# TensorE's order in a state-space layer: written out in the text, with two parts of a product between the steps of a unit

## The chip, the cores and the metric

The kernel runs on one core of a Trainium2 chip. A time is the device time of one execution in microseconds (us); the median of three timed runs stands for a kernel. The engines are named as in the profile: PE (TensorE, matmuls and transposes), DVE (VectorE), ACT (ScalarE), POOL (GpSimd) and SP (SyncE, which only issues DMAs here). Each engine works through its own list of instructions in order; an instruction waits until the results and buffers that it needs are there, and everything behind it on its engine waits too.

## What is computed

One inference step of a small decoder: a state-space layer (S5), then one attention layer. The change touches the S5 layer alone. Its core, for 1024 tokens of a prompt (and 8 x 8 tokens of samples, which start from a given state):

```python
def _s5_layer(x, h0_re, h0_im, ...):
    h = _rms_norm(x, g_pre)
    uz = h @ w_in
    u, z = uz[..., :SSM_WIDTH], uz[..., SSM_WIDTH:]
    y, hr, hi = _s5_scan(u, h0_re, h0_im, log_dt, a_re, a_im, b_re, b_im, c_re, c_im, d_skip)
    y = jax.nn.gelu(y)
    y = y * jax.nn.sigmoid(y @ w_glu + b_glu)
    y = y * jax.nn.silu(z)
    return x + _rms_norm(y @ w_out, g_post), hr, hi
```

`_s5_scan` splits the 1024 channels into 64 groups of 16. Each group has 64 complex states; for every token `h = lambda * h + B u` and `y = Re(C h) + d u`, with `lambda` and `B` made from `log_dt`, `a` and `b`.

## The kernel before

**Layout.** The tokens are laid out as 8 phases x 136 columns: eight neighbouring tokens make one chunk, there are 128 chunks of the prompt and 8 samples (`L` = 8, `W` = 136, `NC` = 128). So a row of a channel has 1088 columns, and the states are carried from chunk to chunk only, by a scan over 128 chunks.

**Products.** `u` and `z` are each made in eight column tiles of 128 channels (`KT` = 8), by `gemm_u(ft)` and `gemm_z(ft)`. One such product has three parts, by phases: `ACH = ((0, 3), (3, 3), (6, 2))` gives 408, 408 and 272 columns. A part is 24 matmuls into one bank `psmm`: for each of 8 slices of the inner dimension three (high x high, high x low, low x high, `mm3`, L147 to L149). ACT copies the bank out (L278, L281), and SP stores the finished row to DRAM (`u_d`, `zs_d`). Weights are split into `whi` (ACT, L140) and `wlo` (L141; DVE, or POOL for the odd tiles of z), two buffers each.

**Matrices of a column tile `ft`.** DVE makes `wb`, `ep` and `fk` from the parameters; PE transposes `ep` four at a time into the one bank `psm` (L342), ACT copies it to `et` (L343); eight small matmuls (L355) give `kp`, ACT copies them (L363), DVE adds the diagonal `dk` that POOL made, and SP places `kp` into `tg` with eight DMAs (L368). POOL makes the tables `cs` of cosines and sines (products `cs` and `m`, then their difference or sum), and four DMAs spread them into `cf` (L386). `cs` has one buffer, `cf` two.

**Units.** A column tile is worked on in three units of 3, 3 and 2 groups, named by their first group: (ft,0), (ft,3), (ft,6). A unit goes through the engines like this: PE multiplies the rows `ug` (read back from `u_d`) by `et` into a bank `psb` (L403); ACT copies the halves crosswise to `tb` (L410, L411); DVE multiplies `psb` by the cosines, POOL `tb` by the sines, DVE adds; DVE scans over the chunks (L418); ACT copies crosswise to `ts` (L425, L426); POOL multiplies `ts`, DVE `psb`, and DVE adds both into the states `hs`; PE adds up `tg` x `ug` (L435) and `fk` x `hs` (L436) in a bank `psa`; ACT puts GELU on it (L437) and behind the third unit SP stores the rows to `y_d`. Nearly all of DVE's and POOL's instructions are recorded on the one line of a helper (`tt`, L205).

**Buffers.** PSUM has two banks `psmm`, two `psa`, three `psb` and one `psm`. `hs` has two buffers, `tb` and `ts` share four.

**What sets the order.** All engines: a scheduler that runs a model of the program and takes, of what is ready, the instruction with the highest priority. The parts on matrices and units are in `tc.high_priority(OFA)`, the products are not, the weights have twice that priority. The text has the matrices of `ft`, then `gemm_u(ft + 2)`, the units of `ft`, and from `ft` = 3 on `gemm_z(ft - 3)`; the last three `gemm_z` stand behind the loads `yr` of the finished rows for the gated unit, and fill the time in which these are fetched and split (`yh` by ACT, L456, `yl` by DVE, L457). The gated unit's matmuls are the first with weights `whi_g`.

Of the kernel before, what the change touches and what calls it, by code (L numbers as in the profile page):

```python
# [10 lines left out]
F32 = mybir.dt.float32  # L11
# [4 lines left out]
ALU = mybir.AluOpType  # L16
# [29 lines left out]
LAG = 3  # L46
SHARE = (0.1, 0.2, 0.3, 0.4)
# [153 lines left out]
def s5_layer(tc, nc, io, wp, bank, cst, gains, ident, sgn, zs_d, u_d, y_d, s2):  # L201
# [5 lines left out]
    with ExitStack() as sx:  # L207
# [58 lines left out]
        def gemm(which, ft, evac, w=None):  # L266
            wh, wl = w or weights(which, ft)
            o = rows.tile([128, NTOK], F32, name=f"{which}t{ft}", tag="row")
            for c, (t0, m) in enumerate(ACH):
# [4 lines left out]
                evac(o[:, t0 * W : (t0 + m) * W], ps)  # L274
            return o

        def gemm_u(ft, w=None):
            nc.sync.dma_start(u_d[ft], gemm("u", ft, lambda o, ps: nc.scalar.activation(o, ps, AF.Copy), w))  # L278

        def gemm_z(ft):  # L280
            nc.sync.dma_start(zs_d[ft], gemm("z", ft, lambda o, ps: nc.scalar.activation(o, ps, AF.Copy)))  # L281

        gemm_u(0, w_first)
        gemm_u(1)


# [28 lines left out]
        units = 0  # L315

        for ft in range(KT):
            with tc.high_priority(OFA):
                gs = slice(ft * 8, ft * 8 + 8)

                pk = pk_all[:, gs, :]
                sb = tp.tile([128, 4, 8, GC], F32, name=f"sb{ft}", tag="sb", bufs=2)
                nc.scalar.dma_start(sb, io["s5_bc"][ft, :, 0:4])
                wb = tp.tile([128, 4, 8, GC], F32, name=f"wb{ft}", tag="wb")
                tt(V, wb[:, 0:2], sb[:, 0:2], bc(bc(wri[:, 0, gs], 2, GC), 1, 2), ALU.mult)
                tt(V, wb[:, 2:4], sb[:, 0:2][:, ::-1], bc(wri[:, 1:3, gs], 3, GC), ALU.mult)
                tt(V, wb[:, 0:2], wb[:, 0:2], wb[:, 2:4], ALU.add)
                V.tensor_scalar(sb[:, 2:4], sb[:, 2:4], sgn, None, op0=ALU.mult)

                ep = tp.tile([128, 8, L, GC], F32, name=f"ep{ft}", tag="ep")  # L330
                tm = tp.tile([128, 8, L, GC], F32, name=f"tm{ft}", tag="tm")
                lrv = pk[:, :, K_LR : K_LR + 8][:, :, ::-1]
                liv = pk[:, :, K_LI : K_LI + 8][:, :, ::-1]
                tt(V, ep, bc(lrv, 3, GC), bc(wb[:, 0], 2, L), ALU.mult)
# [54 lines left out]
            if ft + 2 < KT:  # L389
                gemm_u(ft + 2)  # L390
# [1009 lines left out]
```

## Time and profile before

| | |
|---|---|
| median of three runs | 1499.05 us (1498.17 to 1500.22) |
| profiled execution | 1500.17 us, its span 1498.4 us |
| PE busy over the span | 1415.8 us, 94% |
| DVE / ACT / POOL busy | 935.0 / 718.2 / 493.7 us |
| mean granted clock of PE | 0.982 |
| first unit's matmuls (L403) | 93.16 us from the span's start |
| last outputs of the last unit (L436) | end at 313.5 us |
| first matmul of the gated unit | 328.17 us |

The span runs from the first to the last instruction of the profiled execution; 1.8 us of its time lie outside it. The 94% of PE are a mean over very different stages: the attention behind 328 us is most of the span, and the change doesn't touch it. The layer's stretch, 93 to 328 us, has to be read by itself: how busy each engine is in it, and what ended each wait. In the rows, a bracket `[3.07 <-ACT ut L278]` says that the engine stood idle for 3.07 us ahead of this instruction, and that an ACT instruction of that line ended it. "x2" means two records taken together.

### The profile page before, as it was taken

The numbers are of one execution on the slowest core, as the hardware profiler recorded it, in microseconds if no ns is written. First come the engines' busy times: TensorE is split into PE (matmuls) and PEld (weight loads), VectorE is DVE, ScalarE is ACT, GpSimd is POOL, SyncE is SP. The second block draws the span as 40 slices with busy tenths as digits, with TensorE's granted clock in tenths as the row PEclk, the third lists the DMA queues.
The fourth block names the chain that finished last, engine by engine and source line by source line (L and its number), as shares of the span: only waits on it lengthen the run. The fifth ranks groups of instructions, "written<-read, shape, count | busy, mean of one in ns | idle before, by whom it ended". The sixth has DMA issues, their size and how long they took to land.

```text
span 1498.4 us, 26819 instructions
## 1 busy us (share of the span) xinstructions
PE 1415.8 (94%) x9648; PEld 1145.8 (76%) x9648; DVE 935.0 (62%) x1506; ACT 718.2 (48%) x1424; POOL 493.7 (33%) x473
## 2 busy tenths in 40 slices
PE   4987988899999989999999999999998999998997
PEld 3987978899977889999988877666565665565766
DVE  6877887758755531110122149897888888789545
ACT  5233454454434433332333347676665766576321
POOL 6556565325412132222111012433323233334200
PEclk9999999999999999999999999999999999999999
DMA  5345556674134252232288755979878686754026
GB/s 197 103 129 139 140 126 163 145 251 145 58 106 132 91 224 91 85 123 100 103 314 298 255 201 192 339 284 326 295 257 289 250 308 219 268 190 139 11 82 213
DMA packets 129670, 276.41 MB, mean 184 GB/s; under 512 B 21633, under 2 KB 66562, under 8 KB 129538
## 3 DMA queue, kind: packets, MB, share of 16 engines
q1 hardware_dynamic: 127234, 268.41, 54.0%
q10 hardware_dynamic: 2304, 6.29, 1.3%
q8 instruction: 76, 1.25, 0.3%
q14 instruction: 56, 0.46, 0.1%
HBM read 224.55 MB, written 39.35 MB: 176 GB/s over the span
## 4 chain that ended last, share of the span: by engine, by line
PE 75%; DVE 9%; POOL 5%; DMA 4%; issue 3%; ACT 2%; SPq 1%; DVEq 0%; POOLq 0%; ACTq 0%
PE psmm L147 7%; PE psmm L149 7%; PE psmm L148 7%; PE psqk L147 6%; PE psqk L148 6%; PE psqk L149 6%; PE psa L949 5%; PE psb L1182 5%; PE psb L1164 4%; PE psa L990 4%; PE psqk L1139 3%; PE psqk L1140 2%; DMA cf<-cs 2%; PE psa L147 2%; PE psa L149 2%
## 5 line engine op out<-in xcount | busy, mean ns | idle before, releaser
L1120 POOL TENSOR_TENSOR ql<-q,qh 128x256 fp32r<-128x256 f32 x64 | 62.5, 977 | 285.6 <-ACT qh L1119 246.5
L1141 ACT ACTIVATE F<-psqk,bp 128x384 f32<-128x384 f32 (+2 forms) x192 | 111.3, 580 | 64.6 <-PE psqk L1140 49.2
L1146 DVE TENSOR_TENSOR_SCAN F<-F,maskb 128x256 f32<-128x256 f32 (+3 forms) x128 | 131.2, 1030 | 14.0 <-ACT F L1141 13.6
L1149 POOL TENSOR_TENSOR S<-S,F 128x255 f32<-128x255 f32 (+3 forms) x64 | 100.8, 1574 | 115.7 <-DVE F L1148 22.5
L1142 ACT ACTIVATE S<-psqk,bp 128x384 f32<-128x384 f32 (+2 forms) x192 | 111.4, 583 | 22.7 <-PE psb L1164 22.6
L1164 PE MATMUL psb<-cst,S 128*128 128x128 f32 x576 | 96.7, 285 | 4.4 <-DVE og L1186 3.8
L1164 PEld LDWEIGHTS psb<-cst,S 128*128 128x128 f32 x576 | 67.3, 143 | 35.1 <-issue 20.5
L1148 DVE TENSOR_TENSOR_SCAN F<-F 128x384 f32<-128x384 f32 (+1 forms) x64 | 78.9, 1233 | 20.4 <-ACT F L1141 19.8
L1182 PE MATMUL psb<-at,vr 128*64 128x256 f32 (+1 forms) x640 | 90.0, 369 | 1.2 <-DVE at L1168 1.2
L949 PE MATMUL psa<-vp,sat 128*32 128x256 f32 x1024 | 86.1, 388 | 0.1
L1139 PE MATMUL psqk<-ks,qh 128*128 128x384 f32 (+2 forms) x192 | 77.4, 404 | 6.9 <-DVE ks L1104 5.2
L990 PE MATMUL psa<-kp,qbd 128*32 128x256 f32 x1024 | 75.5, 389 | 0.5 <-PE psb L1164 0.5
L1182 PEld LDWEIGHTS psb<-at,vr 128*64 128x64 f32 x640 | 46.7, 137 | 36.6 <-issue 10.3
L1168 DVE TENSOR_TENSOR at<-psb,maskb 128x384 f32<-128x384 f32 (+3 forms) x128 | 60.3, 478 | 21.3 <-PE psb L1164 20.7
L147 PE MATMUL psmm<-xh,whi_u 128*128 128x408 f32 (+1 forms) x192 | 65.3, 341 | 3.7 <-ACT ut L278 3.1
L147 PE MATMUL psmm<-x,whi_g 128*128 128x408 f32 (+1 forms) x192 | 66.6, 347 | 1.1 <-DVE gt L739 1.1
L943 DVE TENSOR_TENSOR_SCAN sF<-sF 128x513 f32<-128x513 f32 x32 | 44.4, 1388 | 36.1 <-ACT sF L940 35.8
L1139 PEld LDWEIGHTS psqk<-ks,qh 128*128 128x128 f32 x192 | 37.0, 193 | 37.8 <-ACT S L1142 12.8
L1140 PE MATMUL psqk<-ks,ql 128*128 128x384 f32 (+2 forms) x192 | 65.8, 344 | 0.0
L148 PE MATMUL psmm<-xl,whi_u 128*128 128x408 f32 (+1 forms) x192 | 65.4, 341 | 0.0
L149 PE MATMUL psmm<-x,wlo_g 128*128 128x408 f32 (+1 forms) x192 | 64.9, 338 | 0.2 <-DVE wlo_g L141 0.2
L148 PE MATMUL psmm<-x,whi_g 128*128 128x408 f32 (+1 forms) x192 | 65.1, 339 | 0.0
(452 smaller groups left out, 4234.6 us busy)
## 6 DMA issues: line engine op xcount, KB each, us to landing
kp<-cache_kT SPq DMA_DIRECT2D x128, 512.0 KB, 6.0
vp<-cache_v SPq DMA_DIRECT2D x128, 512.0 KB, 5.7
cf<-cs SPq DMA_DIRECT2D x32, 256.0 KB, 5.4
q<-q_d SPq DMA_DIRECT2D x128, 64.0 KB, 4.6
u_d<-ut SPq DMA_DIRECT2D x8, 544.0 KB, 2.8
ug<-u_d SPq DMA_DIRECT2D x64, 68.0 KB, 2.9
y_d<-gt SPq DMA_DIRECT2D x64, 68.0 KB, 2.4
zs_d<-zt SPq DMA_DIRECT2D x8, 544.0 KB, 4.5
```

What stands on the lines that cost most here:

```text
L147: nc.tensor.matmul(ps, sh, mh, start=(k == 0), stop=False)
L148: nc.tensor.matmul(ps, sh, ml, start=False, stop=False)
L149: nc.tensor.matmul(ps, sl, mh, start=False, stop=(k == n - 1))
L949: self.nc.tensor.matmul(po[32 * r : 32 * r + 32, 0:256], a[:, 32 * r : 32 * r + 32], rhs[:, r * 256 : (r + 1) * 256], start=start, stop=stop)
L990: nc.tensor.matmul(ps[32 * r : 32 * r + 32, half * 256 : half * 256 + 256], self.qbd[:, 2 * r + e, s, :], kt[:, :, 2 * r + e, :], start=(e ...
L1139: nc.tensor.matmul(ps[:, :m], qh[:, w], ks[:, c0 : c0 + m], start=True, stop=False)
L1141: nc.scalar.activation(F[:, c0 : c0 + m], ps[:, :m], AF.Sigmoid, bias=bp[:, 1, h : h + 1], scale=-0.125)
L1142: nc.scalar.activation(S[:, c0 : c0 + m], ps[:, :m], AF.Sigmoid, bias=bp[:, 0, h : h + 1], scale=0.125)
L1146: V.tensor_tensor_scan(fr, fr, self.maskb[:, 512 - m : 512][:, ::-1], 1.0, ALU.mult, ALU.max)
L1149: (Q if i % 2 else V).tensor_tensor(S[:, 0 : n - 1], S[:, 0 : n - 1], F[:, 1:n], op=ALU.mult)
L1164: nc.tensor.transpose(ps[:, j * 128 : (j + 1) * 128], S[:, (j0 + j) * 128 : (j0 + j + 1) * 128], self.ident)
L1182: nc.tensor.matmul(po[hs, o:256], self.vr[pi][:, j, hs], ats[hh][j // 4][:, j % 4, o:256], start=(j == 0), stop=(j == nj - 1))
```

## The change

A product becomes a generator that yields after each part, and the products stand in one list: u0, then the order of `FILLS`. From the first product to the end of the layer's units PE takes its instructions in the order of the text (`tc.manual_schedule` for PE alone); the other engines' order still comes from the scheduler, whose model now has PE's order given. `fill(n)` writes the next n parts. The work of a unit is split in two functions: `states` (the matmuls into `psb` and all up to `hs`) and `outputs` (the matmuls into `psa` and GELU). The loop goes over the 24 units: states of unit n, one part of a product, outputs of unit n - 2 (`ULAG` = 2), and behind the second and third unit of a tile one half of the next tile's matrices. In the first three tiles one more part stands ahead of the second half. `hs` has three buffers instead of two, `tb` and `ts` three instead of four.

```diff
+ULAG = 2
+FILLS = "u1 u2 z0 u3 u4 z1 u5 z2 u6 z3 u7 z4 z5 z6 z7".split()
...
-        def gemm(which, ft, evac, w=None):
+        def gemm(which, ft, w=None):
...
-                evac(o[:, t0 * W : (t0 + m) * W], ps)
-            return o
...
-        gemm_u(0, w_first)
-        gemm_u(1)
+                nc.scalar.activation(o[:, t0 * W : (t0 + m) * W], ps, AF.Copy)
+                if c == len(ACH) - 1:
+                    nc.sync.dma_start((u_d if which == "u" else zs_d)[ft], o)
+                yield
+        fills = chain(gemm("u", 0, w_first), *(gemm(n[0], int(n[1])) for n in FILLS))
+        st.enter_context(tc.manual_schedule(engines={mybir.EngineType.PE}))
+        def fill(n):
+            for _ in range(n):
+                next(fills, None)
+        fill(6)
...
-        for i in range(2):
+        for i in range(ULAG + 1):
...
-                    tb = work.tile([128, 3, NC], F32, name=f"tb{ft}_{g0}", tag="tb", bufs=4)
+            tb = work.tile([128, 3, NC], F32, name=f"tb{ft}_{g0}", tag="tb", bufs=3)
...
-                    hs = h_t[units % 2]
+            hs = h_t[(3 * ft + j) % (ULAG + 1)]
...
+        first = matrices(0)
+        fill(7)
+        ahead(first)
+        fill(1)
+        ahead(first)
+        nxt = None
+        for n in range(3 * KT + ULAG):
+            ft, j = divmod(n, 3)
+            if n < 3 * KT:
+                with tc.high_priority(OFA):
+                    states(ft, j)
+            if j == 1 and ft + 1 < KT:
+                nxt = matrices(ft + 1)
+            fill(1)
+            if n >= ULAG:
+                with tc.high_priority(OFA):
+                    outputs(*divmod(n - ULAG, 3))
+            if nxt and j:
+                if j == 2 and ft < 3:
+                    fill(1)
+                ahead(nxt)
+                nxt = nxt if j == 1 else None
...
-        for ft in range(5, 8):
-            gemm_z(ft)
+        for _ in fills:
+            pass
```

`matrices(ft)` holds the text of before in two halves: up to `fk`, with all eight transposes, and from the `kp` products to the loads `ug`. `ahead` runs one half at the high priority.

**How the order moves, first place: POOL at the first unit.** `m2` and `cs2` belong to tile 2's table, `dk1` to tile 1, `tb0_0` and `ts0_0` to the first unit; `wlo_z1` is a weight split. Before:

```order
L205 TENSOR_TENSOR m2_1370<-uu_569 128x512
L205 TENSOR_TENSOR tb0_0_966<-tb0_0_966,cf0_861 128x384
L205 TENSOR_TENSOR cs2_1369<-uu_569 128x512 x2
L205 TENSOR_TENSOR cs2_1369<-cs2_1369,m2_1370 128x512
L205 TENSOR_TENSOR ts0_0_977<-ts0_0_977,cf0_861 128x384
```

After:

```order
L207 TENSOR_TENSOR m2_1643<-uu_571 128x512
L207 TENSOR_TENSOR cs2_1642<-uu_571 128x512 x2
L207 TENSOR_TENSOR cs2_1642<-cs2_1642,m2_1643 128x512
L207 TENSOR_TENSOR m2_1643<-uu_571 128x512
L207 TENSOR_TENSOR dk1_1340<-cst_63,dcol_572 16x128
L207 TENSOR_TENSOR tb0_0_1114<-tb0_0_1114,cf0_1096 128x384
L207 TENSOR_TENSOR cs2_1642<-cs2_1642,m2_1643 128x512
L143 TENSOR_TENSOR wlo_z1_1398<-wraw_z1_1395,whi_z1_1397 128x1024
L207 TENSOR_TENSOR m3_1927<-uu_571 128x512
L207 TENSOR_TENSOR ts0_0_1124<-ts0_0_1124,cf0_1096 128x384
```

The first unit's `tb` has moved behind the first half of tile 2's table and `dk1`, and its `ts` behind the rest of the table and a weight split.

**Second place: PE at the end of column tile 3.** `psa` are outputs, `psb` states, `psm` transposes, `psmm` parts of a product; `hs` and `fk3` belong to tile 3's last unit, `et4` and `ug4` to tile 4's last, `ep5` to the matrices of tile 5. Before:

```order
L147 MATMUL psmm103_2525<-xh0_89,whi_z2_2520 128x408
L342 MATMUL psm92_2279<-cst_63,ep5_2267 128x128
L435 MATMUL psa83_2094<-ug4_2070,tg0_792 128x136
L436 MATMUL psa72_1808<-hs1_790,fk3_1597 128x136
L435 MATMUL psa72_1808<-ug3_1726,tg1_793 128x136
L436 MATMUL psa72_1808<-hs1_790,fk3_1597 128x136
L403 MATMUL psb86_2140<-ug4_2070,et4_1928 128x136 x2
L342 MATMUL psm92_2279<-cst_63,ep5_2267 128x128 x3
L148 MATMUL psmm103_2525<-xl0_92,whi_z2_2520 128x408
```

After:

```order
L151 MATMUL psmm89_2292<-xh0_89,wlo_z3_2288 128x408
L451 MATMUL psa90_2318<-ug3_1939,tg1_797 128x136
L452 MATMUL psa90_2318<-hs2_794,fk3_1808 128x136
L451 MATMUL psa90_2318<-ug3_1939,tg1_797 128x136
L452 MATMUL psa90_2318<-hs2_794,fk3_1808 128x136
L347 MATMUL psm91_2345<-cst_63,ep5_2339 128x128 x4
L347 MATMUL psm92_2351<-cst_63,ep5_2339 128x128 x4
L409 MATMUL psb93_2362<-ug4_2197,et4_2086 128x136 x2
L149 MATMUL psmm94_2382<-xh1_90,whi_z3_2287 128x408
```

Before, the small steps stood singly inside a part of a product; now they stand together between two whole parts, the two sets of transposes back to back.

**Third place: POOL in column tile 5**, with the table of tile 7. Before:

```order
L205 TENSOR_TENSOR ts5_0_2439<-ts5_0_2439,cf5_2323 128x384
L205 TENSOR_TENSOR tb5_3_2458<-tb5_3_2458,cf5_2323 128x384
L205 TENSOR_TENSOR cs7_2917<-uu_569 128x512 x2
L205 TENSOR_TENSOR cs7_2917<-cs7_2917,m7_2918 128x512
L205 TENSOR_TENSOR m7_2918<-uu_569 128x512
```

After:

```order
L207 TENSOR_TENSOR cs7_2958<-uu_571 128x512 x2
L207 TENSOR_TENSOR ts5_0_2478<-ts5_0_2478,cf5_2450 128x384
L207 TENSOR_TENSOR cs7_2958<-cs7_2958,m7_2959 128x512
L207 TENSOR_TENSOR tb5_3_2525<-tb5_3_2525,cf5_2450 128x384
L207 TENSOR_TENSOR m7_2959<-uu_571 128x512
```

The table's first products have moved ahead of the `ts` of unit (5,0). At the end of the layer PE has, behind the last `L436`, 95 matmuls of z products before the gated unit; behind the last `L452` it has 120.

## Rows read from the trace of the kernel before

**Rows 1.** By stretch: length; PE, PEld, DVE, ACT, POOL busy; clock; DMA share; GB/s.
```profile
93.00:310.20 217.20, 188.65 (x1290) 179.59 (x1289) 165.40 (x290) 100.73 (x228) 124.93 (x99) 0.96 0.57 139
131.00:290.50 159.50, 139.06 (x947) 132.11 (x946) 128.33 (x215) 73.16 (x168) 94.40 (x72) 0.96 0.62 148
...
313.30:328.20 14.90, 14.90 (x98) 14.89 (x98) 5.89 (x5) 7.00 (x9) 2.53 (x1) 1.00 0.86 252
...
225.00:250.00 25.00, 20.03 (x132) 19.15 (x131) 18.26 (x35) 9.71 (x23) 13.73 (x12) 0.86 0.63 159
```

**Rows 2.** PE's waits, 93 to 310.2 us: total, times, longest.
```profile
PE psa L435 <- ACT gt L437: 10.0, 4, 5.0
PE psa L436 <- DVE hs L205: 8.4, 4, 3.5
```

**Rows 3.** DVE's waits from 131 to 290.5 us, in the same columns.
```profile
DVE psb L205 <- ACT ts L426: 12.5, 12, 1.1
DVE hs L205 <- POOL ts L205: 4.9, 3, 3.4
DVE psb L205 <- ACT tb L411: 4.2, 10, 0.6
DVE psb L205 <- POOL tb L205: 4.1, 2, 3.2
DVE sb L328 <- DMA sb<-s_bc: 3.2, 2, 1.7
```

**Rows 4.** PE's instructions in order: start us, duration us, name, [idle before <- releaser].
```profile
66.17 0.35 PE L147 MATMUL psmm<-xh,whi_u 128*128 128x408 f32 x1
...
70.63 0.29 PE L147 MATMUL psmm<-xh,whi_u 128*128 128x272 f32 x1
...
73.65 0.35 PE L147 MATMUL psmm<-xh,whi_u 128*128 128x408 f32 x1
...
105.93 0.71 PE L147 MATMUL psmm<-xh,whi_u 128*128 128x408 f32 x1 [3.07 <-ACT ut L278]
...
312.89 0.39 PE L435 MATMUL psa<-ug,tg 128*128 128x136 f32 x2
313.12 0.39 PE L436 MATMUL psa<-hs,fk 128*128 128x136 f32 x2
...
328.17 0.35 PE L147 MATMUL psmm<-yh,whi_g 128*128 128x408 f32 x1
```

**Rows 5.** POOL's instructions at the start, and one of its waits (93 to 310.2 us).
```profile
98.76 1.00 POOL L205 TENSOR_TENSOR tb<-tb,cf 128x384 f32<-128x384 f32 x1
105.92 2.15 POOL L205 TENSOR_TENSOR cs<-uu 128x512 f32<-128x512 f32 x2 [6.16 <-DMA cf<-cs]
108.03 1.28 POOL L205 TENSOR_TENSOR cs<-cs,m 128x512 f32<-128x512 f32 x1
...
115.44 1.51 POOL L205 TENSOR_TENSOR dk<-cst,dcol 16x128 f32<-16x128 f32 x1
...
POOL cs L205 <- DMA cf<-cs: 18.9, 5, 6.2
```

**Rows 6.** DVE's instructions at the first and last units and at the reload.
```profile
99.80 0.57 DVE L205 TENSOR_TENSOR psb<-psb,tb 128x384 f32<-128x384 f32 x1 [3.87 <-POOL tb L205]
...
110.32 0.55 DVE L205 TENSOR_TENSOR hs<-psb,ts 128x381 f32<-128x381 f32 x1 [2.69 <-POOL ts L205]
...
126.42 0.42 DVE L205 TENSOR_TENSOR hs<-psb,ts 128x254 f32<-128x254 f32 x1 [0.37 <-POOL ts L205]
...
290.46 0.28 DVE L205 TENSOR_TENSOR kp<-kp,dk 16x128 f32<-16x128 f32 x1 [0.40 <-ACT kp L363]
...
293.76 0.42 DVE L205 TENSOR_TENSOR hs<-psb,ts 128x254 f32<-128x254 f32 x1 [0.43 <-POOL ts L205]
...
309.68 0.42 DVE L205 TENSOR_TENSOR hs<-psb,ts 128x254 f32<-128x254 f32 x1 [0.43 <-POOL ts L205]
...
327.42 1.29 DVE L457 TENSOR_TENSOR yl<-yr,yh 128x1088 fp32r<-128x1088 f32 x1 [1.18 <-ACT yh L456]
```

More of the change, by code (lines that the diff above doesn't have):

```diff
@@ new lines, in states @@
+        def states(ft, j):
+            g0, n = ACH[j]
+            pk, et, fk, tg, cof, sif = made[ft]
+            ug = rows_in[ft]
+            pg = bank("b")
+            for i in range(n):
+                nc.tensor.matmul(pg[:, i * W : (i + 1) * W], et[:, g0 + i, :], ug[:, g0 + i, :], start=True, stop=True)
+            pg3 = pg[:, : n * W].rearrange("p (a b) -> p a b", a=n)
+            gsl = slice(ft * 8 + g0, ft * 8 + g0 + n)
+            gl = slice(g0, g0 + n)
+            ta = pg3[:, :, 0:NC]
+            tb = work.tile([128, 3, NC], F32, name=f"tb{ft}_{g0}", tag="tb", bufs=3)
+            nc.scalar.activation(tb[0:64, :n], pg3[64:128, :, 0:NC], AF.Copy)
+            nc.scalar.activation(tb[64:128, :n], pg3[0:64, :, 0:NC], AF.Copy, scale=-1.0)
+            tt(V, ta, ta, cof[:, gl], ALU.mult)
+            tt(V, sst[:, gsl, :], pg3[:, :, NC:W], pk[:, gl, K_LH : K_LH + NS], ALU.add)
+            tt(Q, tb[:, :n], tb[:, :n], sif[:, gl], ALU.mult)
+            tt(V, ta, ta, tb[:, :n], ALU.add)
+            for i in range(n):
+                g = ft * 8 + g0 + i
+                V.tensor_tensor_scan(
+                    ta[:, i], rho[:, g : g + 1].to_broadcast([128, NC]), ta[:, i], 0.0, ALU.mult, ALU.add
+                )
+            hs = h_t[(3 * ft + j) % (ULAG + 1)]
+            ts = work.tile([128, 3, NC], F32, name=f"ts{ft}_{g0}", tag="tb", bufs=3)
+            nc.scalar.activation(ts[0:64, :n], ta[64:128], AF.Copy, scale=-1.0)
+            nc.scalar.activation(ts[64:128, :n], ta[0:64], AF.Copy)
+            tt(Q, ts[:, :n], ts[:, :n], sif[:, gl], ALU.mult)
+            nc.scalar.activation(hs[:, :n, NC:W], pk[:, gl, K_H0 : K_H0 + NS], AF.Copy)
+            tt(V, ta, ta, cof[:, gl], ALU.mult)
+            tt(V, hs[:, :n, 1:NC], ta[:, :, 0 : NC - 1], ts[:, :n, 0 : NC - 1], ALU.add)
+            tt(V, l1[:, gsl], ta[:, :, NC - 1], ts[:, :n, NC - 1], ALU.add)
+            started[ft, j] = hs
@@ new lines, in outputs @@
+        def outputs(ft, j):
+            g0, n = ACH[j]
+            gl = slice(g0, g0 + n)
+            pk, et, fk, tg, cof, sif = made[ft]
+            ug, hs = rows_in[ft], started.pop((ft, j))
+            if j == 0:
+                rows_out[ft] = work.tile([128, 8, W], F32, name=f"gt{ft}", tag="gt")
+            gt = rows_out[ft]
+            py = bank("a")
+            for i in range(n):
+                g = g0 + i
+                o = py[:, i * W : (i + 1) * W]
+                nc.tensor.matmul(o, tg[:, g, :], ug[:, g, :], start=True, stop=False)
+                nc.tensor.matmul(o, fk[:, g, 1:, :].rearrange("p a b -> p (a b)"), hs[:, i, :], start=False, stop=True)
+            nc.scalar.activation(gt[:, gl], py[:, : n * W].rearrange("p (a b) -> p a b", a=n), AF.Gelu_apprx_tanh)
+            if j == len(ACH) - 1:
+                ydst = y_d[ft].rearrange("(g c) (t n) -> t c g n", c=GC, t=L)
```

194 lines of the change are left out of this document (77 added, 117 removed).

## The prediction, before the result

> **What bounds the kernel now.** I read the stretches first. Between the first unit's matmuls (93 us) and the end of the last column tile but one or so (310.2 us) TensorE (PE) is busy for 188.65 of 217.2 us, VectorE (DVE) for 165.40, and nobody is full [rows 1]. So the question is who waits for whom. PE's own waits come next: the two largest are for GELU results that free its `psa` bank (10.0 us) and for the states `hs` from DVE (8.4 us) [rows 2]; both are ends of the chain of a unit, which runs PE, ACT, DVE, POOL, DVE, ACT, POOL, DVE, PE. PE stands because that chain is late, not because its own queue is badly filled. Then DVE's waits from the end of tile 1's `kp` to the start of tile 7's (131 to 290.5 us): 12.5 us for the copy `ts` and 4.2 us for the copy `tb`, both in small pieces, one for nearly every unit; and, in a few long pieces, 4.9 us for POOL's `ts`, 4.1 us for POOL's `tb`, 3.2 us for the load `sb` [rows 3]. The first kind lies inside a unit (scan, then copy by ACT, then multiply) and I call it structural; the second kind, 4.9 + 4.1 + 3.2 = 12.2 us, could go with another order. DVE is busy for 128.33 of these 159.5 us [rows 1]; with the structural waits, and some 2 us that no row names, that is 159.5 - 12.2 = 147.3 us, 24.5 us for a column tile. PE in the same window has 139.06 us of work [rows 1]. My reading: the chain through DVE sets the pace of the units, and the products fill PE beside it. What is left of the products runs behind the last unit: from 313.1 us to the first matmul of the gated unit at 328.17 us, without a gap (14.90 us busy of 14.90) [rows 1, 4].
>
> So the end of the layer is: time at which the last unit's outputs are through, plus the products still to do then. After that the order of the program is the same in both kernels, and I carry any difference through unchanged.
>
> **The change, part by part.**
>
> *The start (+1.3).* Before, POOL does the first unit's `tb` at 98.76 us, ahead of the table `cs` of tile 2, which it can only start at 105.92 us, after 6.16 us of waiting for tile 1's `cf` transfers to read the single `cs` buffer [rows 5]. After, four instructions of tile 2's table and tile 1's `dk` stand ahead of that `tb` on POOL (the first fence of the change). With the same landing, `tb` starts at about 105.92 + 2.15 (two products) + 1.28 (the difference) + 1.1 (one more product, half of the pair) + 1.51 (`dk`) = 112 us [rows 5], 13 us later. Behind it, the last step of the table and one weight split stand ahead of `ts`, some 5 us; the first `hs` comes at about 119 us where it came at 110.32 [rows 6]. PE in text order then stands at the first outputs for about 8 us, and everything behind waits: next unit's part, tile 1's transposes. Most of it is covered: DVE does tile 1's matrices while it waits, which before stood between the units, and its waits there (3.87 us ahead of 99.80, 2.69 us ahead of 110.32 [rows 6]) are partly the same idle time. Walking DVE's list with the durations of the trace I get the third unit's `hs` at about 128.9 us for 126.42, and tile 1's `kp` at the old time but with 1.3 us of work still behind it that was ahead of it. Bounds: 0 (all hidden) and 119 - 110.3 = 8.9 us (none). I take 1.3, since DVE has the work to hide it.
>
> *Six column tiles (-5).* From one `kp` to the next DVE has the same instructions. PE gets a state matmul of a unit out two units before its outputs, so DVE no longer waits for one; DVE had hardly such a wait before. What can shrink are the 12.2 us. They shrink where POOL's order is better: in tiles 1 to 3 the tables stand together between two units. In tiles 4 and 5 it gets worse: the two first products of `cs6` and `cs7`, 2.15 us a pair as at 105.92 [rows 5], and the rest of the table, stand ahead of a `ts` that DVE wants next (the third fence shows tile 5). Walked by hand: 1.0 us left in tile 1, 0.5 in tile 3, 1.8 in tile 4, 2.7 in tile 5, and 0 to 3 for `sb`, together 6 to 9 of the 12.2. The gain is 3.2 to 6.2 us; I take 5. Bounds: 12.2 (all gone), and a loss of 4.45 us, if one unit's matmuls come behind a whole part of a product at a point where DVE is waiting: a part of 408 columns took 70.63 - 66.17 = 4.46 us, one of 272 columns 73.65 - 70.63 = 3.02 us [rows 4].
>
> *PE's own budget.* A tile has three parts (4.45 + 4.45 + 3.0 = 11.9 us), or four in the first three tiles, and about 7 us of its own: 24 matmuls of the units at 313.12 - 312.89 = 0.23 us [rows 4], 5.5, and 16 smaller ones for the matrices, some 1.5. That is 18.9 or 23 us, less than the 24.5 of DVE. Both transposes of a tile now come back to back through the one `psm` bank, so PE waits for ACT's copy between them, at most 1.3 us a tile. With 5.6 us to spare in tiles 3 to 7 this costs nothing; without that cover (tiles 0 to 2, 1.5 us to spare) it would cost those 1.3 us once or twice. So PE still idles, about 5 us in each late tile, now always in one place, ahead of the outputs.
>
> *The last unit (-1).* Before, from tile 6's last `hs` (293.76 us) to the last output (313.12 + 0.39 us) went 19.75 us [rows 4, 6]. After, PE has behind that `hs`: outputs 0.9, states 0.45, a part 4.45, outputs 1.4, a part 3.0, outputs 1.4, a part 4.45, outputs 0.9, that is 17, and a wait of about 1.5 for the last `hs`, since DVE took 309.68 - 293.76 = 15.9 us for the same three units [rows 6]. I take 18.7, a gain of 1; bounds 0 and 2.7.
>
> *What is left behind the last output (+4.45).* The text hands out 14 parts before the first unit, one in each of 26 rounds and one more in three: 43 of 48. Five are left, two of z6 and three of z7, 120 matmuls where 95 stood before: 14.9 + 4.45 = 19.35 us. This is a count, with no range of its own. It hides the reload of the layer's result, whose last split stood at 327.42 us, about the end of z7 [rows 6], a little better than before.
>
> Sum: 1.3 - 5 - 1 + 4.45 = -0.25 us. The profiled execution took 1500.17 us with a span of 1498.4; the median of the three timed runs is 1499.05, 1.1 us below it. Against the median I get **1498.8 us**: no change. About 0.2%, 3 us, is what a measurement of this kernel can tell from none.
>
> **A rule to weigh.** The rows show two busy engines in the units, PE at 188.65 and DVE at 165.40 of 217.2 us [rows 1], and PE's waits naming DVE and ACT [rows 2]. The Trainium skill, page "Perfetto Trace Analysis", section "Identifying the Most-Contended Engine", holds the engine with the highest occupancy to be the one to work on first, though it adds that for TensorE busy time is a poor measure. By that rule PE would be the limit, and a better order on PE would pay its whole idle time. The sum above does not use it; it is the third rival below.
>
> **The rivals.**
>
> *DVE's avoidable waits go altogether (faster).* If the two units between states and outputs let POOL run ahead everywhere, all 12.2 us go and the start costs nothing: -12.2 - 1 + 4.45 = -8.7, about 1490 us. For it: POOL is busy for only 94.40 of 159.5 us [rows 1], so it has room. Against it: its order, and 18.9 us of waiting of POOL for `cf` transfers that still read the single `cs` [rows 5].
>
> *The units end no earlier (slower).* If the start's slip is not hidden, or PE's fixed order returns what POOL gives, the last output stays at 313.5 us or comes later, and the 4.45 us of products that were moved behind it are simply added: 1503.5 us, and up to 1508 with half of the 8.9 us of the start on top. The point at which it decides: units that get shorter by less than 4.45 - 3 = 1.5 us give a measurable loss. For it: PE in text order stands at every outputs that is late, and has nothing to put ahead of it. A worse form of it: the granted clock. After an idle time of 3.07 us the next matmul of 408 columns took 0.71 us instead of 0.35 [rows 4], and 225 to 250 us, with PE's longest wait of 5.0 us [rows 2], shows a granted clock of 0.86 [rows 1]. If every late tile's wait of 5 us does so, each brings some us of matmuls at 1.2 GHz; only where PE has no spare time does that reach the end, so I price it at 0 to 5 us inside this rival.
>
> *PE is the limit (much faster).* If PE's order alone made the waits, the 217.2 - 188.65 = 28.6 us of idle time go, less the first outputs' 8: 1499 - 20.6, about 1478 us. Against it: the waits end with DVE and ACT [rows 2]. The Trainium skill's rule above is this case.
>
> *The order does not matter.* PE's idle time is what DVE's pace leaves, wherever it lies; some 8 us at the start and five times 5 us are about 33, less what the units end earlier, near the 28.6 of before. This is the forecast by another way.
>
> **How the numbers follow.** No change (within 3 us of 1499): 0.38. DVE's waits gone: 0.25, PE the limit: 0.07, and a forecast whose tile term comes out at its better end, 0.02: faster 0.34. Units end no earlier: 0.20 without and 0.08 with the clock: slower 0.28. The range takes the first rival with some 4 us beyond it, as the ends of the terms (-12.2, -2.7) add up, 1485, and the slower one with its upper end, 1508. Left out are the limit by PE and tails on both sides, together about 0.2. The likeliest case's own range is 1496 to 1502.
>
> **What would show it.** In the changed kernel's profile: POOL's first `tb` near 112 us and PE's longest wait ahead of the first outputs, for `hs`; tile 7's `kp` on DVE at 285 to 288 us where it was 290.46 [rows 6]; the last outputs near 309 us and the first gated matmul near 328, with about 19.3 us of PE without a gap between; PE's waits by name nearly all `hs` from DVE, some `et` from ACT. If PE's idle time in the units falls well below 28 us, I am wrong about what bounds them; if the last outputs come at 313 us or later, the slower case holds; if the first gated matmul waits for anything but PE, the tail was mis-sized.

## The result, and the profile after

The changed kernel takes 1510.47 us (median of four timed runs, 1507.9 to 1512.5) against 1499.12 us of the kernel before on the same chip: a ratio of 1.0075, with a 95% interval of 1.0055 to 1.0094. It is slower by 11 us; the prediction said 1498.8, with a range that ended at 1508. The profiled execution took 1508.97 us with a span of 1507.2 us, 8.8 us more than the span before.

Where these 8.8 us come in is read off these marks in the two traces (us from the span's start; an `hs` is marked where DVE starts to write it):

| mark | before | after | difference so far |
|---|---|---|---|
| first states (psb <- ug, et) | 93.16 | 95.66 | +2.5 |
| hs of unit (6,6) | 293.76 | 291.21 | -2.55 |
| last outputs end | 313.5 | 314.8 | +1.3 |
| first gated matmul | 328.17 | 334.00 | +5.8 |
| the next PE wait of over 4 us | 540.19 | 549.22 | +9.0 |
| end of the span | 1498.4 | 1507.2 | +8.8 |

So DVE's chain is ahead of the old one near its end, and yet the layer ends later; then another 3.2 us are lost between the first gated matmul and the next long wait. The busy times of two stretches of the changed kernel, in the columns of [rows 1]:

```profile
95.60:314.50 218.90, 183.00 (x1255) 177.45 (x1249) 162.51 (x289) 99.00 (x227) 118.69 (x94) 0.94 0.53 135
314.50:334.00 19.50, 19.50 (x123) 19.49 (x122) 8.99 (x6) 8.92 (x12) 2.54 (x1) 1.00 0.87 283
```

In the units PE now stands for 218.9 - 183.0 = 35.9 us; before it was 28.6 [rows 1], in a stretch of nearly the same length. The second line is the tail: 19.5 us without a gap, where 14.9 stood [rows 1]. PE's waits of the changed kernel from 85 to 340 us, to be read against [rows 2]:

```profile
PE psm L347 <- ACT et L348: 28.4, 8, 8.0
PE psa L452 <- DVE hs L207: 3.7, 3, 2.4
PE psb L409 <- DVE wb L207: 2.6, 1, 2.6
PE psb L409 <- DMA ug<-u_d: 2.0, 1, 2.0
```

Of the two large waits of before, the one for GELU is gone, and the one for `hs` is down from 8.4 to 3.7 us. One new wait holds nearly all: at the second set of transposes of each tile PE stands for ACT's copy of the first set out of the one `psm` bank. One such place, in tile 3's matrices, from PE's list (start, duration, instruction, idle time ahead of it):

```profile
164.57 0.60 PE L347 MATMUL psm<-cst,ep 128*128 128x128 f32 x4
169.70 1.11 PE L347 MATMUL psm<-cst,ep 128*128 128x128 f32 x4 [4.53 <-ACT et L348]
170.61 1.11 PE L409 MATMUL psb<-ug,et 128*128 128x136 f32 x4
171.36 0.70 PE L149 MATMUL psmm<-xh,whi_z 128*128 128x408 f32 x1
```

The last two rows, the next unit's states and the next part of a product, did not need that copy; in the order of the text they had to stand behind it. Why the copy was late is in ACT's list at the same time:

```profile
165.42 0.49 ACT L429 ACTIVATE ts<-psb 64x384 f32<-64x384 f32 x1 [4.67 <-DVE psb L424]
165.92 0.48 ACT L430 ACTIVATE ts<-psb 64x384 f32<-64x384 f32 x1
166.43 0.49 ACT L416 ACTIVATE tb<-psb 64x384 f32<-64x384 f32 x1
166.93 0.48 ACT L417 ACTIVATE tb<-psb 64x384 f32<-64x384 f32 x1
167.43 1.06 ACT L142 ACTIVATE whi_u<-wraw_u 128x1024 fp32r<-128x1024 f32 x1
168.39 0.38 ACT L277 ACTIVATE ut<-psmm 128x272 f32<-128x272 f32 x1
168.67 0.39 ACT L453 ACTIVATE gt<-psa 128x272 f32<-128x272 f32 x1
168.95 0.22 ACT L432 ACTIVATE hs<-pk 128x16 f32<-128x16 f32 x1
169.05 0.60 ACT L348 ACTIVATE et<-psm 128x512 f32<-128x512 f32 x1
```

The copy takes 0.60 us, but eight other instructions stand ahead of it, and the first of them waits 4.67 us for a scan on DVE (L424). A transpose that needs nothing of the units has come to wait for the unit in work. In four of the eight places the copy stood behind a scan like this. The longest wait, 8.0 us ahead of tile 1's second transposes, had another reason: ACT also issues the loads of u's weights, and one of them could only go when POOL had split the weights of z out of the one buffer `wraw`.

```profile
109.48 2.33 POOL L143 TENSOR_TENSOR wlo_z<-wraw_z,whi_z 128x1024 fp32r<-128x1024 f32 x1
...
111.84 0.33 ACTq L222 DMA_DIRECT2D wraw_u<-a_win  x1
112.22 0.51 ACT L277 ACTIVATE ut<-psmm 128x408 f32<-128x408 f32 x1 [11.33 <-POOL wlo_z L143]
```

(Counted in the loop, three parts stand between a unit's states and its outputs, in the rounds n, n + 1 and n + 2, and not the two of the title.)

### The profile page after: what moved, and what is told of

Same layout as the page of the kernel before. It is cut to its first block, busy times and chain, and to the rows that moved or that the text cites. A ratio compares the mean times of both kernels' runs of the same rounds, so it can differ in the third digit from the quotient of the medians.

```text
span 1507.2 us, 26829 instructions
## 1 busy us (share of the span) xinstructions
PE 1417.8 (94%) x9648; PEld 1150.1 (76%) x9648; DVE 925.2 (61%) x1507; ACT 716.4 (48%) x1424; POOL 491.0 (33%) x473
## 4 chain that ended last, share of the span: by engine, by line
PE 73%; DVE 6%; DMA 4%; issue 2%; POOL 2%; ACT 2%; SPq 1%; DVEq 0%; POOLq 0%; ACTq 0%
PE psmm L149 6%; PE psmm L151 6%; PE psmm L150 6%; PE psqk L150 6%; PE psqk L149 6%; PE psqk L151 6%; PE psa L992 5%; PE psb L1225 5%; PE psa L1033 4%; PE psb L1207 4%; PE psqk L1182 3%; PE psqk L1183 2%; PE psa L149 2%; PE psa L151 2%; PE psa L150 2%
## 5 line engine op out<-in xcount | busy, mean ns | idle before, releaser
L1225 PEld LDWEIGHTS psb<-at,vr 128*64 128x64 f32 x640 | 46.7, 137 | 36.1 <-issue 10.5
L149 PE MATMUL psmm<-xh,whi_z 128*128 128x408 f32 (+1 forms) x192 | 66.7, 347 | 0.0
L986 DVE TENSOR_TENSOR_SCAN sF<-sF 128x513 f32<-128x513 f32 x32 | 44.4, 1388 | 36.1 <-ACT sF L983 35.8
```

The lines of the kernel that those rows point to most:

```text
L149: nc.tensor.matmul(ps, sh, mh, start=(k == 0), stop=False)
L1225: nc.tensor.matmul(po[hs, o:256], self.vr[pi][:, j, hs], ats[hh][j // 4][:, j % 4, o:256], start=(j == 0), stop=(j == nj - 1))
```

## The experiments

Each kernel is the changed one with the edit shown, or one of these with a further edit. "Ratio" is against the kernel before, with its 95% interval. The table has, for all, what the trace of the profiled execution shows: PE's idle time between the first states and the last outputs, the largest of its waits there, and three marks. The kernel before was timed again beside each group of runs, so two runs are best compared by their ratios. A last run, x12_units_alone, was timed once and stands in the text only.

| run | median us | ratio | PE idle | largest waits | hs (6,6) | last outputs | first gated matmul |
|---|---|---|---|---|---|---|---|
| before | 1498.6 to 1500.1 | 1 | 28.6 | GELU 10.0, hs 8.4 | 293.8 | 313.5 | 328.2 |
| after | 1510.5 | 1.0075 [1.0055, 1.0094] | 35.9 | et 27.6 | 291.2 | 314.8 | 334.0 |
| x1_other_bank | 1522.8 | 1.0145 [1.0122, 1.0167] | 47.0 | ug 21.2, hs 15.7 | 291.8 | 328.7 | 347.9 |
| x2_apart | 1516.0 | 1.0108 [1.0084, 1.0132] | 38.3 | hs 10.2, ug 9.6 | 292.3 | 322.2 | 341.4 |
| x3_three_left | 1512.1 | 1.0070 [1.0045, 1.0095] | 33.4 | et 26.9 | 296.2 | 321.1 | 332.9 |
| x4_bank_and_three | 1507.3 | 1.0050 [1.0034, 1.0067] | 33.0 | ug 18.0, hs 10.6 | 294.5 | 318.3 | 330.1 |
| x6_bank_early_rows | 1511.8 | 1.0084 [1.0067, 1.0100] | 35.5 | hs 24.9 | 293.6 | 319.5 | 338.7 |
| x15_half_parts | 1513.2 | 1.0088 [1.0071, 1.0105] | 40.5 | et 23.7, hs 13.7 | 299.8 | 323.6 | 345.0 |
| x17_no_parts_at_end | 1507.5 | 1.0056 [1.0038, 1.0075] | 36.6 | et 28.4 | 293.1 | 310.1 | 335.9 |
| x13_free_z | 1505.5 | 1.0041 [1.0028, 1.0054] | 29.6 | et 12.4, hs 11.8 | 290.1 | 310.2 | 334.5 |
| x5_free_order | 1499.1 | 1.0000 [0.9990, 1.0010] | 25.9 | hs 6.2, GELU 6.0 | 291.6 | 311.2 | 327.8 |
| x14_steps_fixed | 1496.2 | 0.9985 [0.9975, 0.9994] | 24.2 | hs 6.5, ep 5.2 | 292.4 | 311.8 | 326.5 |
| x16_steps_and_bank | 1491.6 | 0.9948 [0.9930, 0.9966] | 22.2 | ug 8.0, hs 6.2 | 285.9 | 305.9 | 320.6 |

**Is the transposes' wait the loss?** The first theory took PE's list for the limit through its largest wait. Two edits take that wait away.

```diff
-                ps = bank("m")
+                ps = bank("a" if i else "m")
                 for j in range(4):
```

> The changed kernel with one edit: a tile's second set of transposes goes into a psa bank instead of the one psm bank, so that it no longer waits for ACT's copy of the first set. Theory A (PE is the limit between 95 and 314 us, through its 28.4 us of waits at the second transposes): these waits fall under 5 us, waits for hs rise to 5 to 12 us because DVE becomes last, the last outputs end 6 to 14 us earlier than 314.8 us, and the time falls from 1510 to 1496 to 1504 us. Theory B (the chain through DVE sets the pace, and PE would stand elsewhere): the waits turn up again at the outputs for hs, 20 us or more, and the time stays within 3 us of 1510.

The wait is gone, as wanted, and the kernel is 12 us slower still (10 to 11 by the ratios), an outcome that neither theory had. PE's waits, then one of its rows, in this run:

```profile
PE psb L409 <- DMA ug<-u_d: 21.2, 3, 13.5
PE psa L452 <- DVE hs L207: 15.7, 5, 7.9
...
298.40 0.56 PE L409 MATMUL psb<-ug,et 128*128 128x136 f32 x1 [13.51 <-DMA ug<-u_d]
```

PE now stands at the states for the rows `ug`. The 13.5 us are tile 7's; SP's list shows why:

```profile
282.33 0.60 SPq L392 DMA_DIRECT2D cf<-cs  x1
282.97 0.60 SPq L279 DMA_DIRECT2D u_d<-ut  x1
287.26 2.67 SPq L398 DMA_DIRECT2D ug<-u_d  x6
290.03 5.17 SPq L374 DMA_DIRECT2D tg<-kp  x8
295.24 1.06 SPq L398 DMA_DIRECT2D ug<-u_d  x2
```

The row `u7` is stored at 283 us behind a table's transfer, and two of the eight loads of it stand behind tile 7's eight `tg` transfers. Each engine's list is fixed ahead of the run; a list that is a little out of step with PE's now stops PE, which has nothing that it may take instead. One mark says more than the total: the `hs` of unit (6,6) comes at 291.8 us, with 40.4 of the 47.0 us of idle time ahead of it, and at 291.2 us in the changed kernel, with 35.9. Up to there the units came no earlier without the old wait, and no later with the new ones. Behind it the wait for tile 7's rows does hold the units: the last `hs` comes at 318.2 us where it came at 306.2, with the same 19.2 us of products behind the last outputs.

```diff
                 nc.scalar.activation(et[:, 4 * i : 4 * i + 4, :], ps.rearrange("p (a b) -> p a b", a=4), AF.Copy)
+                if i == 0:
+                    yield
...
         ahead(first)
+        ahead(first)
         fill(1)
...
             fill(1)
+            if nxt and j == 2:
+                ahead(nxt)
             if n >= ULAG:
```

> The changed kernel with one edit: the second set of transposes stands one part of a product later (behind the next unit's states and a part), in the same psm bank. Theory A: the waits at transposes fall from 28.4 to under 6 us, and the time falls as with the other bank, to 1496 to 1504 us; a wait moves to the third unit's states only where the second et copy is late. Theory B: within 3 us of 1510.

The same: 1516.0 us, the wait at the transposes down to 8.2 us (with 4.1 us more at the `kp` products, which need the same bank), and `hs`, `ug` and `tg` in its place. The theory that this one wait is the loss falls.

**Is it what was moved behind the last unit?**

```diff
-                if j == 2 and ft < 3:
+                if j == 2 and ft < 5:
```

> The changed kernel with two more parts handed out inside the units (column tiles 3 and 4 get a fourth part), so that three instead of five are left behind the last outputs: 11.9 instead of 19.4 us. Theory C (what was moved behind the last unit is what costs): the last outputs stay within 2 us of 314.8, the first gated matmul comes 5 to 7 us earlier, and the time falls by 3 to 7 us. Theory A: PE is the limit, so the last outputs come some 7 us later, the first gated matmul stays at 334, and the time is the same within 3 us, or worse where the reload of the rows is no longer covered.

The tail goes from 19.2 to 11.8 us, and the last outputs come 6.3 us later; the first gated matmul moves by only 1.1 us, as theory A had it. Parts that are taken from the end and put into the units come back nearly whole as longer units. The gated unit then loses what was won: from its first matmul to the next long wait of PE it takes 218.9 us, with a tail of 11.8 us, against 215.2 in the changed kernel and 212.0 before. With the other bank besides:

```diff
-                ps = bank("m")
+                ps = bank("a" if i else "m")
...
-                if j == 2 and ft < 3:
+                if j == 2 and ft < 5:
```

> Both edits: second transposes in a psa bank, and three parts left behind the last outputs. Theory A with DVE next in line: inside the units the two parts fill PE's new waits for hs, the first gated matmul comes 3 to 7 us earlier than with the other bank alone, 1492 to 1500 us; if the reload of the rows (about 15 us from the last outputs) then ends last, the gated unit waits up to 4 us and the time equals that of the other bank alone. Theory B: 1505 to 1512.

1507.3 us: 7 us above the range of theory A and inside that of theory B. Against the changed kernel that is 3 us less, but the intervals of the two ratios overlap. And the other way round, no part at all in the last four rounds:

```diff
-            fill(1)
+            fill(n < 22)
             if n >= ULAG:
```

> The changed kernel without a part in the last four rounds: nine instead of five parts are written behind the units, where the scheduler may put single matmuls of them between the last outputs. If the end of the layer is PE's start plus its work plus its idle time, the first gated matmul stays within 2 us of 334.0, though the last outputs come 5 to 9 us earlier than 314.8; what is gained is the reload of the rows alone, up to 3.5 us: 1506 to 1511 us. If the whole parts between the last units' steps are the loss: the first gated matmul comes 5 us earlier or more, and the time is 1505 us or less.

The last outputs come 4.7 us earlier, the first gated matmul 1.9 us later, the gated unit is back at 211.2 us, and the time is 3 us less than that of the changed kernel, with intervals that overlap. That the first gated matmul comes at PE's start plus its work plus its idle time is bookkeeping, since PE has no gap behind the last outputs. What the run shows is that moving the last parts changes the idle time hardly (36.6 us for 35.9), and so gains nothing up to the first gated matmul; the reload behind it gains 4.0 us.

**Does PE stand for the rows because of SP?** With the other bank, and the loads written at the start of a tile's matrices (and taken out at their end):

```diff
         def matrices(ft):
+            ug = work.tile([128, 8, W], F32, name=f"ug{ft}", tag="ug")
+            usrc = u_d[ft].rearrange("(g c) (t n) -> t c g n", c=GC, t=L)
+            for t in range(L):
+                nc.sync.dma_start(ug[t * GC : (t + 1) * GC], usrc[t])
+            rows_in[ft] = ug
```

> The run with the other bank, and the loads of a tile's rows ug written at the start of its matrices instead of the end. Theory F (with the transposes' wait gone PE stood for the ug loads, 21.2 us, since SP had them behind kp's transfers and the rows to store): this wait falls under 8 us and the time from 1522.8 to 1500 to 1510 us. Rival G (SP's list hardly changes, as the two ug buffers come free only with the outputs two units later): the wait stays above 12 us and the time above 1512.

The wait for `ug` goes and the time falls to 1511.8 us, just outside the expected range. What PE waits for now:

```profile
PE psa L452 <- DVE hs L207: 24.9, 8, 7.8
PE psa L451 <- ACT gt L453: 6.0, 2, 5.7
```

These are the two waits of [rows 2] again, at 31 us instead of 18. With transposes and rows out of the way the chain through DVE is what PE stands for, and its idle time, 35.5 us, is that of the changed kernel: the time that PE loses has only changed its name.

**Is it the fixed order itself?** One line out, all else of the change kept (lag, buffers, text):

```diff
-        st.enter_context(tc.manual_schedule(engines={mybir.EngineType.PE}))
```

> The changed kernel without the fixed order: the same text, lags and buffers, but the scheduler orders PE as it does the other engines. Theory D (a list in the order of the text stands with ready products behind each late step, and that is the whole loss; the lag of two units, three hs and three tb buffers cost nothing): PE's idle time between 95 us and the last outputs falls from about 41 to 25 to 30 us and the time to 1497 to 1502 us. Rival E (lag and buffers lose it: rows held longer, tb and ts in three buffers): 1507 us or more.

1499.08 us against 1498.76: no difference, with an interval of 0.1% on both sides. The expectation's "about 41" us counts the idle time from the first product on; over the stretch that it names the changed kernel has 35.9, and this run 25.9. With PE's order free the three `hs` buffers, the three `tb` buffers and the lag of two units cost nothing; the loss of the change is the fixed order of PE. Its waits are many and small:

```profile
PE psa L451 <- DVE hs L207: 6.2, 3, 4.2
PE psa L450 <- ACT gt L452: 6.0, 2, 4.4
PE psmm L149 <- ACT ut L277: 4.4, 2, 3.4
PE psm L346 <- DVE ep L207: 3.1, 2, 2.7
```

**The grain of the parts, or their fixed place?** Parts cut in two halves of 12 matmuls:

```diff
                     mm3(nc, ps, wh[:, k, :], wl[:, k, :], mh, ml, k, KT)
+                    if k == 3:
+                        yield
...
-        fill(6)
+        fill(12)
...
-        fill(7)
+        fill(14)
         ahead(first)
-        fill(1)
+        fill(2)
...
                     outputs(*divmod(n - ULAG, 3))
+            fill(1)
             if nxt and j:
                 if j == 2 and ft < 3:
-                    fill(1)
+                    fill(2)
```

> The changed kernel with its parts cut in halves of 12 matmuls: one half ahead of a round's outputs and one behind them, the same number of matmuls ahead of, between and behind the units. Theory D with grain as its cause (a whole part of 4.45 us is too coarse): waits at the second transposes fall by some 2 us each, from 28.4 to about 14, and the time to 1500 to 1506 us. If only the fixed place matters and not the grain: waits stay at 35 us or more in all and the time within 3 us of 1510.

1513.2 us, idle time 40.5 us. A finer grain at fixed places doesn't help. The next run has the u products in the text and all z products behind the units, where the scheduler may put their matmuls between the fixed steps:

```diff
-FILLS = "u1 u2 z0 u3 u4 z1 u5 z2 u6 z3 u7 z4 z5 z6 z7".split()
+FILLS = "u1 u2 u3 u4 u5 u6 u7 z0 z1 z2 z3 z4 z5 z6 z7".split()
...
-            fill(1)
+            fill(n < 10)
             if n >= ULAG:
...
-                if j == 2 and ft < 3:
-                    fill(1)
```

> The changed kernel with the u products alone in the text (all u first, one part in each of the first ten rounds); every z product is written behind the units, outside the fixed order, so the scheduler may put single z matmuls between the fixed steps. Theory D (what costs is that whole parts stand at fixed places and nothing can be put ahead of a late step): from column tile 3 on PE's waits fall under 10 us in all, and the time is 1492 to 1502 us. Theory B in its strict form (the chain's pace is the same, wherever PE's idle time lies): the stretch from the first states to the last outputs stays at 215 to 222 us and some 25 us of z products stand behind it: 1510 to 1520 us.

1505.5 us, between the two expected ranges. The units' stretch is 208.8 us instead of 219, though its first units start 5.7 us later, behind more of the u products; 24.3 us of products stand behind it. A run with all u products ahead of the units and all z products free, timed once, was meant to measure the units alone:

```diff
-        fill(7)
+        fill(17)
...
-            fill(1)
             if n >= ULAG:
```

> A measurement of the chain's own pace: all eight u products are done ahead of the first unit and no part of a product stands between the units; all z products stand behind them. The stretch from the first states to the last outputs then has only the units' own work on PE, some 55 us. Theory B (the chain through DVE sets the pace): the stretch takes 195 to 220 us, as in the changed kernel (219). Theory A (PE in its fixed order sets it): under 170 us. The whole time says little here: with B it is 1560 to 1600 us, since 24 z parts (some 95 us) stand behind.

It didn't measure that: the scheduler put 574 of the 576 z matmuls between the first states and the last outputs, so PE was not empty. The stretch took 198.1 us, inside the range of theory B, but with 163.7 us of work on PE it doesn't tell the two theories apart. The whole took 1516.2 us. (This diff leaves out the reordered list and the extra part, as in the run before.) Last, the fixed order kept inside each step only, with the products free:

```diff
-        st.enter_context(tc.manual_schedule(engines={mybir.EngineType.PE}))
+        fixed = lambda: tc.manual_schedule(engines={mybir.EngineType.PE})
...
-                with tc.high_priority(OFA):
+                with fixed(), tc.high_priority(OFA):
                     states(ft, j)
...
-                    outputs(*divmod(n - ULAG, 3))
+                with fixed(), tc.high_priority(OFA):
+                    outputs(*divmod(n - ULAG, 3))
```

> The changed kernel with the fixed order only inside each step (a unit's states, a unit's outputs, half of a tile's matrices: each keeps its matmuls in the order of the text), while the parts of the products are left to the scheduler. If the products' fixed places are what costs: PE's idle time between the first states and the last outputs is 24 to 30 us, the wait at the second transposes goes, and the time is 1497 to 1502 us as in the run with the free order. If fixing the steps themselves costs: 1504 us or more.

1496.2 us, a ratio of 0.9985 [0.9975, 0.9994]: a little faster than the kernel before and than expected. With free products the other bank is worth trying again:

> The run with only the steps fixed, and a tile's second transposes in a psa bank. If the one psm bank holds units back even where products can fill PE's waits: 1492 to 1495 us. If the transposes' wait was never on the chain of the units (as the times of the states hs with and without it, 291.2 and 291.8 us, suggest): 1495 to 1500 us, no gain.

1491.6 us, a ratio of 0.9948 [0.9930, 0.9966], the fastest of all, and 0.5% faster than the kernel before. The same edit that cost 10 to 12 us in the fixed order gains some 5 in the free one. PE's waits in it:

```profile
PE psb L409 <- DMA ug<-u_d: 8.0, 4, 3.5
PE psa L452 <- DVE hs L207: 6.2, 3, 4.7
PE psm L347 <- DVE ep L207: 4.2, 3, 2.4
PE psmm L149 <- ACT zt L277: 2.3, 2, 1.3
```

The rows `ug` are waited for here too, but for 8 us instead of 21, in four pieces of at most 3.5 us. My second expectation, no gain, was wrong: the `hs` of unit (6,6) comes at 285.9 us where the run without the bank has 292.4. That the bank alone did this isn't shown, since the scheduler ordered all engines anew.

## Why the prediction was wrong, step by step

In the profiled executions the terms of the sum came out like this:

| term | predicted | measured | from |
|---|---|---|---|
| start, to hs of (0,6) | +1.3 | +0.65 | 127.07 for 126.42 us |
| six column tiles, hs of (0,6) to (6,6) | -5 (-3.2 to -6.2) | -3.2 | 164.14 for 167.34 us |
| last unit | -1 | +3.8 | 23.57 for 19.76 us |
| products left behind | +4.45 | +4.6 | 19.22 for 14.65 us |
| behind the layer | 0 | +3.2 | 549.22 - 334.00 for 540.19 - 328.17 |
| sum | -0.25 | +9.0 | |

**What held.** The first two terms and the tail were right to 2 us. POOL's first `tb` came at 107.3 us instead of the predicted 112, since the transfers that POOL waits for had landed 5 us earlier, and PE did stand for 8.0 us there, only one step further up, at tile 1's transposes.

**What is not shown** is the reading behind these terms, that the chain through DVE, and not PE, sets the pace of the units. Taking one wait of PE for another did leave the `hs` of unit (6,6) at 291.2 to 292.3 us in three kernels (after, x1, x2). But the six column tiles, 164.1 us in the changed kernel, took 171.2 with half parts (x15), 150.8 with the z products free (x13) and 155.4 with the steps fixed and the other bank (x16), so the pace does change with what stands in PE's list. Differences of 2 us say nothing here: x17, which has the text of the changed kernel up to its last rounds, took 166.0.

**The step that failed** is "PE's own budget": that PE waits "at most 1.3 us a tile" at the second transposes and that "this costs nothing". It was 28.4 us in eight places, up to 8.0 us. I took the wait to be ACT's copy and left out ACT's queue: eight instructions ahead of the copy in the place shown, the first of them waiting for a scan. And I checked only whether PE's spare time covers the wait within a tile. But what PE does not do in that time it does at the end: from the last of these waits, which ends at 278.18 us, PE has no wait in the changed kernel until the gated unit, so idle time ahead of that point stands in full ahead of the first gated matmul. These two rows, before and after, run from the first matmul of u0 to the first gated matmul and hold the same matmuls:

```profile
23.18:328.17 304.99, 268.86 (x1769) 257.90 (x1770) 232.74 (x438) 130.52 (x278) 166.46 (x153) 0.96 0.55 139
23.44:334.00 310.56, 269.28 (x1768) 261.22 (x1769) 233.97 (x439) 130.72 (x280) 162.55 (x153) 0.96 0.52 141
```

PE's busy time is the same to 0.4 us; the idle time is 41.3 us for 36.1, 5.2 us longer. With a start 0.3 us later that makes the measured 5.8. The granted clock is 0.96 over the stretch in both, but not in the same places: it is 0.94 for 0.96 in the units [rows 1] and 1.00 for 0.93 ahead of them. So in this pair of executions the loss up to the first gated matmul is PE's waiting. That the waits at the transposes by themselves are the loss is refuted above (x1, x2, x6); what is shown is that the fixed order makes PE wait longer, for whatever is late: with the products free to move, its idle time in the units is 25.9 us (x5) and 24.2 us (x14) for 35.9.

**The last unit** is the term with the largest error. I let PE follow DVE's `hs`. These two rows of DVE,

```profile
291.21 0.41 DVE L207 TENSOR_TENSOR hs<-psb,ts 128x254 f32<-128x254 f32 x1
...
306.22 0.42 DVE L207 TENSOR_TENSOR hs<-psb,ts 128x254 f32<-128x254 f32 x1 [0.39 <-POOL ts L207]
```

show that DVE took 15.0 us from unit (6,6) to the last unit, less than the 15.9 of before [rows 6]. But PE was not in step with it:

```profile
272.88 0.50 PE L452 MATMUL psa<-hs,fk 128*128 128x136 f32 x2 [0.20 <-DVE hs L207]
...
278.18 0.79 PE L347 MATMUL psm<-cst,ep 128*128 128x128 f32 x4 [3.91 <-ACT et L348]
...
297.59 0.39 PE L451 MATMUL psa<-ug,tg 128*128 128x136 f32 x2
...
313.68 0.39 PE L451 MATMUL psa<-ug,tg 128*128 128x136 f32 x2
...
334.00 0.35 PE L149 MATMUL psmm<-yh,whi_g 128*128 128x408 f32 x1
...
342.32 0.45 PE L150 MATMUL psmm<-yl,whi_g 128*128 128x408 f32 x1 [1.97 <-DVE yl L500]
```

At the outputs of unit (5,6) it waited 0.20 us for the `hs`; then it stood for 3.91 us at tile 7's transposes, and it came to the outputs of (6,6) only at 297.59 us, 6.4 us after DVE started on their `hs`. From there its list took 17.2 us, for the 17 of the prediction, and 6.4 + 17.2 is the measured 23.6. PE came to the last outputs (313.68 us) 7.0 us after their `hs` was there. It was like that in most of the changed kernel: over the 24 units PE's `hs` matmuls started 5.5 us (median) after the `hs` was done, before 0.9 us. The whole parts at their fixed places have their share in it: without parts in the last four rounds (x17) the last `hs` matmuls start 0.9 us after their `hs`.

The last of these rows is the step on **the reload**, where I expected a slightly better cover. The first gated matmul waits for nothing, as predicted, but the thirty-third waits 1.97 us for the last split `yl`, and the next 7.7 us run at a lower granted clock:

```profile
342.30:350.00 7.70, 7.68 (x41) 7.57 (x42) 3.57 (x5) 2.26 (x5) 0.00 (x0) 0.78 0.62 221
```

At 0.78 these 7.7 us hold 1.7 us of lost clock; with a wait of 1.97 us where the only one of the kernel before, for another operand, was 0.50 us, that makes the 3.2. I had looked at the first matmul of the next stage only, not at the operand that comes last.

**The rival that came true** is "the units end no earlier", given 0.28: the last outputs are 1.3 us late and the 4.6 us of products are added. Its mechanism held in part: PE in text order had nothing to put ahead of a late step, but it stood at the second transposes (28.4 us) and hardly at the outputs (3.7 us for `hs`), and its worse form, the clock, shows ahead of the gated unit only in the 0.94 of the units, which the stretch ahead of them made up for. Its upper end, 1508, lacked the gated unit's 3.2 us. The line "the order does not matter", by which PE's idle time is what DVE's pace leaves, is refuted by the run with the free order: 25.9 us against 35.9 with the same text. And the rival by which PE is the limit failed as it was priced: no order that was run came below 1491.6 us, where it had 1478. The Trainium skill, page "Perfetto Trace Analysis", section "Identifying the Most-Contended Engine", would have the engine with the highest occupancy worked on first. The trace agrees in one sense, with PE as that engine: once the last units are reached PE is busy without a break, and 5.2 of the 5.8 us lost up to the gated unit are its idle time before.

**What stays open.** Why single lists came out of step (tile 7's loads behind `tg`, the tables of tile 2 ahead of the first unit) was read off the traces, not tried one by one. Why PE's idle time is shorter with free products was not followed wait by wait, and what sets the pace of the units, DVE's chain or PE's list, stays open. So does what the lower clock in the units costs by itself: as an estimate from the two stretches, 0.06 of 219.1 us less 0.04 of 220.4, some 4 us if PE had been busy throughout. The medians lie 11.4 us apart and the profiled executions 8.8; only the 8.8 were followed.

## What to carry to other kernels

An order written out for one engine is only as good as the lists of the others: where five engines feed each other, each late step stops all that stands behind it, and taking away the largest wait brings up the next. Fix the order inside the steps that belong together, and leave work that needs nothing (here the products) free to be put ahead of a late step; that was the difference between 1510 and 1496 us, and it let a further edit gain that had cost 10 to 12 us before. When a wait "costs nothing" because another engine sets the pace, ask whether the waiting engine will be the last one to finish: then its idle time is only put off, not covered. And price a wait for another engine by that engine's queue, not by the one instruction waited for.

## What the hardware showed that I had not expected

In the kernel before, the shortest wait that I had used as one behind which the granted clock falls was 3.07 us [rows 4]. In the changed kernel it fell behind shorter ones: 0.78 over the 7.7 us behind the wait of 1.97 us in the gated unit (the row stands above), and 0.78 over the 7.8 us behind another wait of 1.97 us, for `et` at 141.29 us. But behind a wait of 1.96 us, for `ug` at 235.24 us, it stayed at 1.00. So the length of a wait of about 2 us doesn't tell by itself whether the clock falls. The stretches behind the other two waits:

```profile
141.20:149.00 7.80, 7.71 (x49) 7.71 (x50) 4.90 (x9) 1.14 (x4) 3.96 (x3) 0.78 0.73 161
235.20:243.00 7.80, 7.76 (x59) 7.78 (x60) 7.80 (x13) 4.12 (x9) 4.11 (x3) 1.00 0.21 41
```
